# 1/rms on GpSimd by a power, its diagonal products on ScalarE, and a bound that joins the next product, in a one-core encoder block

## The chip, the cores and the metric

The kernel runs on one core of a Trainium2 chip. A core has TensorE (matrix products, PE in the profile; PEld is its loading of weights), VectorE (DVE), ScalarE (ACT), GpSimd (POOL) and SyncE (SP, which here only starts transfers). The metric is the device time of one execution in microseconds; compared are medians of several runs.

## The reference

Two inputs, one of 512 tokens and one of 1024, pass through one encoder layer of width 1024, all in 32-bit floats:

```
h    = rmsnorm(x, norm_mix);   q, k, v, xr, gate = split(h @ w_in)
o    = rmsnorm(diff_attention(q, k, v), subln_g) * 0.8        # 4 heads of 128
xc   = depthwise conv of width 4 over tokens of xr
hl   = rg_lru(xc, forward) + rg_lru(xc, backward)
x    = x + concat(o, hl * gelu(gate)) @ w_out
h2   = rmsnorm(x, norm_ffn)
x    = x + (silu(h2 @ w_gate) * (h2 @ w_up)) @ w_down
out  = rmsnorm(x, norm_final)

rmsnorm(x, g) = x * rsqrt(mean(x * x) + 1e-6) * g
rg_lru: r, i = sigmoids of block products of xc;  a = exp(-8 r softplus(-lambda))
        h_t = a_t h_(t-1) + sqrt(max(1 - a_t^2, 1e-12)) * i_t * xc_t
```

## The kernel before

Activations lie transposed: features on the 128 partitions, tokens along the columns, in blocks of 512 tokens (block 0 is the short input, 1 and 2 the long one). Each 32-bit operand is split into a high part and a remainder (ScalarE rounds, `wh`, `xh`, `hp`; VectorE or GpSimd subtracts, `wl`, `xl`), and each product is three matmuls (`mm3`, L222 to L224).

The work is staged so that TensorE always has a dense product: the input projection of block 0 (`proj`) with the attention of the short input (`attention`) and the recurrent branch (`lru`) beside it; the input projection of blocks 1 and 2; the output projection (`out_proj`); gate and up projections of the short input beside the attention of the long one; then the long input's feed-forward part with sums of halves (`pair_products`), whose sums and differences GpSimd makes (`minus`, L691); and the down projection with the final norm (`finish`). The side work is written as generators that `advance` steps by costs set by hand. That gives the order of the program text; each engine's queue is then laid out by the framework when the kernel is built, by its own scheduling, so that instructions of other stages stand between those of one function. Each engine runs its queue in order.

The norm is made in the same way at 18 places. For the ten RMS norms, squares are added up by VectorE, and `inv_rms_cols` brings the sum over features to one column for each 128 tokens by tiny matmuls with ones (`ss`, L288). VectorE scales it and adds 1e-6 (`ve`, L290). `rsqrt_cols` makes 1/sqrt from it with an integer guess and three Newton steps: eleven VectorE operations on 2, 4 or 8 columns (`rs`, `rt`, L257 to L262). The eight head norms of the attention make their own mean (`ov`, L570) and call `rsqrt_cols` too. `bcast_cols` turns each column into a diagonal matrix (VectorE, `dg`, L270, two buffers) and multiplies it by a matrix of ones (TensorE, `bc`, L271), which gives 1/rms along the tokens on all partitions.

In `lru`, VectorE bounds 1 - a^2 from below (L463), ScalarE takes the root with a factor 0.25 under it (L464, with a load of another table ahead), and VectorE multiplies (L466) and scans (L469).

Of the kernel before, what the change touches and what calls it, by code (L numbers as in the profile page):

```python
# [11 lines left out]
F32 = mybir.dt.float32  # L12
F32R = mybir.dt.float32r
I32 = mybir.dt.int32
F16 = mybir.dt.float16
AF = mybir.ActivationFunctionType
ALU = mybir.AluOpType
# [3 lines left out]
P = 128  # L21
D = 1024
# [8 lines left out]
EPS = 1e-6  # L31
# [57 lines left out]

def build(tc, io, es):  # L90
    nc = tc.nc
    V, A, T = nc.vector, nc.scalar, nc.tensor
    VG = (nc.vector, nc.gpsimd)

    def pool(stack, name, bufs=1, **kw):
        return stack.enter_context(tc.tile_pool(name=name, bufs=bufs, **kw))

    cp = pool(es, "const")
# [11 lines left out]
    def small(n, name, bufs=2):  # L110
        return smp.tile([P, n], F32, name=name, tag=name, bufs=bufs)
# [8 lines left out]
    def bank(name, tag):  # L120
        return banks[tag].tile([P, BLK], F32, name=name, tag=tag)
# [13 lines left out]
    ident = cp.tile([P, P], F32, name="ident")  # L135
    nc.scalar.dma_start(ident, io["ident"])
    onesq = cp.tile([P, P], F32, name="onesq")
    V.memset(onesq, 1.0)
    ones = onesq[:, 0:1]

    warm = cp.tile([P, 1], F32, name="warm")
    A.activation(warm, ones, AF.Exp)
# [6 lines left out]
    def split(h, l, src, eng=V):  # L149
        A.copy(h, src)  # L150
        eng.tensor_tensor(l, src, h.bitcast(F32), ALU.subtract)  # L151
# [68 lines left out]
    def mm3(out, wh, wl, ah, al, first, last, more=False):  # L220

        T.matmul(out, lhsT=wh, rhs=ah, start=first, stop=False, skip_group_check=more)  # L222
        T.matmul(out, lhsT=wh, rhs=al, start=False, stop=False, skip_group_check=more)  # L223
        T.matmul(out, lhsT=wl, rhs=ah, start=False, stop=last, skip_group_check=more)  # L224
# [28 lines left out]
    def rsqrt_cols(ve, n, who="m"):  # L253

        r = small(n, f"rs{who}{n}")
        t = small(n, f"rt{who}{n}")
        V.tensor_scalar(t.bitcast(I32), ve.bitcast(I32), 1, None, ALU.arith_shift_right)  # L257
        V.tensor_scalar(r.bitcast(I32), t.bitcast(I32), -1.0, float(0x5F375A00), ALU.mult, ALU.add)
        for _ in range(3):
            V.tensor_tensor(t, r, r, ALU.mult)  # L260
            V.scalar_tensor_tensor(t, t, -0.5, ve, ALU.mult, ALU.mult)
            V.scalar_tensor_tensor(r, t, 1.5, r, ALU.add, ALU.mult)  # L262
        return r

    def bcast_cols(tag, r, c0, who="m", n=4):

        bc = bank("bc", tag)
        for i in range(n):
            dg = small(P, "dg")
            V.tensor_scalar(dg, ident, r[:, c0 + i:c0 + i + 1], None, ALU.mult)  # L270
            T.matmul(bc[:, i * P:(i + 1) * P], lhsT=onesq, rhs=dg, start=True, stop=True)  # L271
        return bc[:, 0:n * P]

# [10 lines left out]
    def inv_rms_cols(tag, acc, n=4):  # L284

        ss = bank("ss", tag)
        for i in range(n):
            T.matmul(ss[:, i:i + 1], lhsT=acc[:, i * P:(i + 1) * P], rhs=ones, start=True, stop=True)  # L288
        ve = small(n, f"ve{n}")
        V.tensor_scalar(ve, ss[:, 0:n], 1.0 / D, EPS, ALU.mult, ALU.add)  # L290
        return rsqrt_cols(ve, n)

    def inv_rms(tag, acc, n=4):

        return bcast_cols(tag, inv_rms_cols(tag, acc, n), 0, n=n)
# [11 lines left out]
    def load_block(b, other=None, xring="raw"):  # L307
# [32 lines left out]
        if b == 0:  # L340
            for c in range(KC):
                square(c)
        r = inv_rms_cols("lru", acc)
        if b:
            yield YL
        bc = bcast_cols("lru", r, 0)
        rows[b] = rings["rows"](HALF, f"rms{b}")
        A.copy(rows[b], bc)
# [55 lines left out]
    def lru(s, ready):  # L404
        n = length[s]
        nb = n // BLK
        z = n / SEQ_S

        for _ in range(4):
            while not ready:  # L410
                yield 0.5
            c, xr, gt = ready.pop(0)
            gr = rings["lh"]((P, 4, P), "gr")
            nc.sync.dma_start(gr, io["w_gates"][c].rearrange("p (k m) -> p k m", k=4))
            gh = rings["lh"]((P, 4, P), "gh", F32R)
            gl = rings["lh"]((P, 4, P), "gl", F32R)
            split(gh, gl, gr)
            xc = rings["lru"]([P, n], "xcv")

            def col(o):  # L420
                return par[:, o:o + 1]

            A.activation(xc, xr[:, 0:n], AF.Identity, scale=col(C_CW + 4 * c), bias=col(C_CB + c))
            for j in range(1, 4):
                V.scalar_tensor_tensor(xc, xr[:, j:j + n], col(C_CW + 4 * c + j), xc, ALU.mult, ALU.add)
                yield 1.5 * z
            xh = rings["lru"]([P, n], "xch", F32R)
            xl = rings["lru"]([P, n], "xcl", F32R)
            split(xh, xl, xc)
            yield 1.2 * z  # L430
            hs = []
            for dirs in ((0, 1),) if n == BLK else ((0,), (1,)):
                m = len(dirs)

                def tiles(name):
                    t = rings["lru"]([P, m, n], name)
                    return t, [t[:, i] for i in range(m)]


                t2, tr = tiles("tr")  # L440
                b2, bv = tiles("ti")
                for i, d in enumerate(dirs):
                    k = 4 * d + c
                    for b in range(nb):
                        w = slice(b * BLK, (b + 1) * BLK)
                        for t, g, o in ((tr, 0, 0), (bv, 1, 8)):
                            pr = bank("pr", "lru")
                            mm3(pr, gh[:, 2 * d + g], gl[:, 2 * d + g], xh[:, w], xl[:, w], True, True)
                            A.activation(t[i][:, w], pr, AF.Tanh, scale=0.5, bias=hb[:, k + o:k + o + 1])
                            yield YG  # L450
                a2, av = tiles("a")
                for i, d in enumerate(dirs):
                    k = 4 * d + c
                    A.activation(av[i], tr[i], AF.Exp, scale=n4sp[:, k:k + 1], bias=n4sp[:, k:k + 1])
                    A.activation(tr[i], tr[i], AF.Tanh, scale=p4sp[:, k:k + 1], bias=p4sp[:, k:k + 1])
                    V.scalar_tensor_tensor(bv[i], bv[i], 1.0, xc, ALU.add, ALU.mult)
                    for b in range(nb):
                        w = slice(b * BLK, (b + 1) * BLK)
                        sq = rings["lh"](HALF, "sqg")
                        A.activation(sq, av[i][:, w], AF.Square)  # L460
                        V.scalar_tensor_tensor(tr[i][:, w], sq, 1.0, tr[i][:, w], ALU.add, ALU.mult)
                    yield 2.0 * z
                V.tensor_scalar(t2, t2, 1e-12, None, ALU.max)  # L463
                A.activation(t2, t2, AF.Sqrt, scale=0.25)  # L464
                yield 1.0 * z
                V.tensor_tensor(b2, b2, t2, ALU.mult)  # L466
                for i, d in enumerate(dirs):
                    o = slice(None, None, -1) if d else slice(None)
                    V.tensor_tensor_scan(bv[i][:, o], av[i][:, o], bv[i][:, o], 0.0, ALU.mult, ALU.add)  # L469
                hs += bv  # L470
                yield 1.9 * z * m
            V.tensor_tensor(hs[0], hs[0], hs[1], ALU.add)

            ge = rings["lru"]([P, n], "ge")
            A.activation(ge, gt, AF.Square)
            V.scalar_tensor_tensor(ge, ge, 1.0 / GELU_A, gt, ALU.add, ALU.mult)
            A.activation(ge, ge, AF.Tanh, scale=GELU_C * GELU_A)
            V.scalar_tensor_tensor(ge, ge, 1.0, gt, ALU.add, ALU.mult)
            yield 3.0 * z
            V.scalar_tensor_tensor(ge, hs[0], 0.5, ge, ALU.mult, ALU.mult)  # L480
            nc.scalar.dma_start(cat[s][4 + c], ge)
            yield 2.7 * z
# [9 lines left out]
    def attention(s, done, vo):  # L492
# [3 lines left out]
        for hd in range(NH):  # L496
# [112 lines left out]
            yield YV  # L609
            late.pop()()  # L610
            r = rsqrt_cols(ve, nk, "a")
            yield YV * z
            for g in range(n // BLK):
                w = slice(g * BLK, (g + 1) * BLK)
                bc = bcast_cols("pv", r, 4 * g, "a")
                V.scalar_tensor_tensor(ot[:, w], ot[:, w], subg, bc, ALU.mult, ALU.mult)
                nc.scalar.dma_start(cat[s][hd][:, w], ot[:, w])
                yield 1.5
# [68 lines left out]
    def parts_of(rs, w):  # L687
        return [Part(f"b{i}{w}", r, w) for i, r in enumerate(rs)]
# [148 lines left out]
    n = (B1 + B2 + 3 + GRP) // 2  # L837
# [91 lines left out]
    b11, b21, b22, t4, t1, t2, t3 = parts_of(["main"] * 4 + ["pg"] * 3, BLK)  # L929
# [305 lines left out]
```

## Time and profile before

| | |
|---|---|
| median of 3 runs | 1801.11 us (1796.82 to 1801.77) |
| profiled execution | 1798.27 us, its span 1796.5 us |
| TensorE, loading of weights | 1743.1 us (97%), 1434.9 us (80%) |
| VectorE, ScalarE, GpSimd | 1331.4 us (74%), 827.2 us (46%), 256.5 us (14%) |
| mean granted clock of TensorE | 0.989 |

The span is the time from the first to the last instruction of one execution that the profiler recorded. A busy share is an average over stages that are limited by different things. Ends of matmuls are modelled and matmuls overlap, so TensorE's 97% is a share of time with work in it. The granted clock is the share of full speed at which TensorE was allowed to run.

### The profile page before, as it was taken

What the parts mean: (1) busy time and instruction counts of PE and PEld (TensorE: products, weight loads), DVE (VectorE), ACT (ScalarE), POOL (GpSimd) and SP (SyncE); (2) the same over time, 40 slices, a digit from 0 to 9 for tenths busy, and PEclk for the clock granted to TensorE, in tenths of its full rate; (3) what the DMA queues carried; (4) which work ended last, traced back from release to release, by engine and by line L of the source; (5) the groups of instructions that cost most, each with busy time, mean ns of one, the idle gap of its engine ahead of it and who ended that gap; (6) DMA issues with size and microseconds to landing.
All of it is one profiled execution on the core that took longest, in us unless ns stands there. A gap on an engine that the chain in (4) does not pass through costs nothing.

```text
span 1796.5 us, 22898 instructions
## 1 busy us (share of the span) xinstructions
PE 1743.1 (97%) x8316; PEld 1434.9 (80%) x8316; DVE 1331.4 (74%) x2154; ACT 827.2 (46%) x1327; POOL 256.5 (14%) x165
## 2 busy tenths in 40 slices
PE   8999999999999999999999979999999999998997
PEld 7777787777888888888788768888888888887797
DVE  6789878777587778786544996767766766989884
ACT  6568556665355545554323432332233334444451
POOL 0000000000000000000000362323322310555200
PEclk9999999999999999999999989999999999999998
DMA  8633424153473222222555642223332239532361
GB/s 291 198 102 111 142 87 135 66 179 119 145 218 114 86 89 93 70 88 71 196 167 180 205 142 100 100 94 106 110 108 100 100 122 369 170 112 70 99 207 54
DMA packets 105026, 238.79 MB, mean 133 GB/s; under 512 B 12240, under 2 KB 21200, under 8 KB 104912
## 3 DMA queue, kind: packets, MB, share of 16 engines
q1 hardware_dynamic: 76608, 185.04, 32.3%
q10 hardware_dynamic: 28304, 52.28, 7.6%
q8 instruction: 65, 1.06, 0.2%
q14 instruction: 49, 0.40, 0.1%
HBM read 180.00 MB, written 57.28 MB: 132 GB/s over the span
## 4 chain that ended last, share of the span: by engine, by line
PE 79%; DVE 10%; ACT 4%; issue 3%; DMA 3%; POOL 1%; ACTq 0%; SPq 0%; DVEq 0%; POOLq 0%
PE gu L222 5%; PE gu L224 4%; PE gu L223 4%; PE pm L223 4%; PE pm L222 4%; PE pm L224 4%; PE acc L223 3%; PE acc L222 3%; PE acc L224 3%; PE y L224 3%; PE y L222 3%; PE y L223 3%; PE sc L591 2%; PE po L223 2%; PE sc L592 2%
## 5 line engine op out<-in xcount | busy, mean ns | idle before, releaser
L222 PE MATMUL pm<-xh,wh 128*128 128x512 f32 x480 | 189.9, 396 | 5.7 <-ACT wh L209 3.3
L223 PE MATMUL pm<-xl,wh 128*128 128x512 f32 x480 | 189.2, 394 | 1.1 <-DVE xl L336 1.1
L224 PE MATMUL pm<-xh,wl 128*128 128x512 f32 x480 | 189.1, 394 | 0.3 <-DVE wl L210 0.3
L209 ACT CAST wh<-wr 128x1024 fp32r<-128x1024 f32 x100 | 104.8, 1048 | 148.5 <-PE gu L223 62.4
L151 POOL TENSOR_TENSOR ws<-wr,ws 128x512 fp32r<-128x512 f32 x8 | 12.7, 1582 | 1013.2 <-ACT ws L150 1013.2
L223 PE MATMUL acc<-hp,ws 128*128 128x512 f32 (+1 forms) x396 | 142.8, 361 | 6.3 <-DVE hp L151 6.3
L222 PE MATMUL acc<-hp,ws 128*128 128x512 f32 (+1 forms) x396 | 143.2, 362 | 2.8 <-ACT hp L150 2.8
L224 PE MATMUL acc<-hp,ws 128*128 128x512 f32 (+1 forms) x396 | 142.5, 360 | 0.6 <-DVE ws L151 0.6
L222 PE MATMUL gu<-yh,wh 128*128 128x512 f32 x352 | 142.0, 403 | 0.9 <-DVE ev L384 0.9
L224 PE MATMUL gu<-yh,wl 128*128 128x512 f32 x352 | 139.0, 395 | 0.0
L223 PE MATMUL gu<-yl,wh 128*128 128x512 f32 x352 | 138.6, 394 | 0.0
L210 DVE TENSOR_TENSOR wl<-wr,wh 128x1024 fp32r<-128x1024 f32 x100 | 122.2, 1222 | 17.6 <-ACT wh L209 16.9
L597 ACT ACTIVATE pb<-pb,mn 128x1024 f32<-128x1024 f32 (+1 forms) x96 | 96.9, 1009 | 73.5 <-DVE mn L594 73.4
L151 DVE TENSOR_TENSOR hp<-hr,hp 128x512 fp32r<-128x512 f32 (+1 forms) x143 | 111.0, 787 | 26.3 <-ACT hp L150 22.4
L594 DVE CUSTOM_DVE_ANT_0 pb<-sc,tab 128x1024 f32<-128x1024 f32 (+1 forms) x96 | 100.1, 1043 | 33.1 <-PE sc L592 31.6
L713 ACT CAST ws<-s 128x512 fp32r<-128x512 f32 x88 | 54.7, 622 | 131.1 <-PE y L224 48.1
L222 PEld LDWEIGHTS pm<-xh,wh 128*128 128x128 f32 x480 | 90.6, 189 | 24.5 <-ACT wh L209 3.5
L150 ACT CAST hp<-hr 128x512 fp32r<-128x512 f32 (+1 forms) x143 | 77.2, 550 | 71.0 <-PE acc L224 24.1
L223 PEld LDWEIGHTS pm<-xl,wh 128*128 128x128 f32 x480 | 90.5, 189 | 19.8 <-DVE xl L336 1.8
L224 PEld LDWEIGHTS pm<-xh,wl 128*128 128x128 f32 x480 | 90.6, 189 | 19.4 <-DVE wl L210 1.0
L713 ACT CAST ws<-wr 128x512 fp32r<-128x512 f32 x66 | 41.1, 622 | 111.1 <-PE y L224 38.2
L223 PEld LDWEIGHTS acc<-hp,ws 128*128 128x128 f32 x396 | 76.3, 193 | 18.1 <-DVE hp L151 7.4
(271 smaller groups left out, 4604.6 us busy)
## 6 DMA issues: line engine op xcount, KB each, us to landing
wr<-w_gate SPq DMA_DIRECT2D x44, 512.0 KB, 3.5
wr<-w_up SPq DMA_DIRECT2D x44, 512.0 KB, 3.5
wr<-w_in SPq DMA_DIRECT2D x40, 512.0 KB, 4.1
hr<-hs SPq DMA_DIRECT2D x77, 256.0 KB, 2.8
hs<-t ACTq DMA_DIRECT2D x44, 256.0 KB, 2.0
hs<-ht ACTq DMA_DIRECT2D x33, 256.0 KB, 2.9
wr<-w_out SPq DMA_DIRECT2D x16, 512.0 KB, 3.6
xd<-xh ACTq DMA_DIRECT2D x28, 256.0 KB, 2.5
```

The source lines that it names most:

```text
L150: A.copy(h, src)
L151: eng.tensor_tensor(l, src, h.bitcast(F32), ALU.subtract)
L209: A.copy(h, r)
L210: V.tensor_tensor(l, r, h.bitcast(F32), ALU.subtract)
L222: T.matmul(out, lhsT=wh, rhs=ah, start=first, stop=False, skip_group_check=more)
L223: T.matmul(out, lhsT=wh, rhs=al, start=False, stop=False, skip_group_check=more)
L224: T.matmul(out, lhsT=wl, rhs=ah, start=False, stop=last, skip_group_check=more)
L591: T.matmul(sc[:, w], lhsT=qh[m][:, qs], rhs=K[m][:, w], start=True, stop=False)
L592: T.matmul(sc[:, w], lhsT=ql[m][:, qs], rhs=K[m][:, w], start=False, stop=True)
L594: V.tensor_tensor_reduce(out=pp[m], in0=sc, in1=tab[:, 896 - q0:896 - q0 + n], scale=-0.125, scalar=3e38, op0=ALU.add, op1=ALU.min, accum_ ...
L597: A.activation(pp[m], pp[m], AF.Exp, scale=-1.0, bias=mn, accum_out=zz)
L713: A.copy(h[:, 0], src)
```

## The change

1/rms is now made by GpSimd: a power with the exponent -0.5 from a constant tile, and one Newton step, five operations in place of eleven on VectorE. The scaling ahead of it (`ve`) and the diagonal products move from VectorE to ScalarE. In the recurrent branch the bound is no longer an operation of its own under the root: the root's result, which carries a factor of a half, is bounded by 5e-7 in the product that follows. Two constants are set at the start.

```diff
+    V, A, T, G = nc.vector, nc.scalar, nc.tensor, nc.gpsimd
...
+    eps = cp.tile([P, 1], F32, name="eps")
+    V.memset(eps, EPS)
+    mhalf = cp.tile([P, 8], F32, name="mhalf")
+    V.memset(mhalf, -0.5)
...
-        V.tensor_scalar(t.bitcast(I32), ve.bitcast(I32), 1, None, ALU.arith_shift_right)
-        V.tensor_scalar(r.bitcast(I32), t.bitcast(I32), -1.0, float(0x5F375A00), ALU.mult, ALU.add)
-        for _ in range(3):
-            V.tensor_tensor(t, r, r, ALU.mult)
-            V.scalar_tensor_tensor(t, t, -0.5, ve, ALU.mult, ALU.mult)
-            V.scalar_tensor_tensor(r, t, 1.5, r, ALU.add, ALU.mult)
+        G.tensor_tensor(r, ve, mhalf[:, 0:n], ALU.pow)
+        G.tensor_tensor(t, r, r, ALU.mult)
+        G.tensor_tensor(t, t, ve, ALU.mult)
+        G.tensor_scalar(t, t, -0.5, 1.5, ALU.mult, ALU.add)
+        G.tensor_tensor(r, t, r, ALU.mult)
...
-            V.tensor_scalar(dg, ident, r[:, c0 + i:c0 + i + 1], None, ALU.mult)
+            A.activation(dg, ident, AF.Copy, scale=r[:, c0 + i:c0 + i + 1])
...
-        V.tensor_scalar(ve, ss[:, 0:n], 1.0 / D, EPS, ALU.mult, ALU.add)
+        A.activation(ve, ss[:, 0:n], AF.Identity, scale=1.0 / D, bias=eps)
...
-                V.tensor_scalar(t2, t2, 1e-12, None, ALU.max)
                 A.activation(t2, t2, AF.Sqrt, scale=0.25)
...
-                V.tensor_tensor(b2, b2, t2, ALU.mult)
+                V.scalar_tensor_tensor(b2, t2, 5e-7, b2, ALU.max, ALU.mult)
```

## Rows read from the trace of the kernel before

**Rows 1.** The page: busy time, share of the span and instructions of each engine.

```profile
PE 1743.1 (97%) x8316; PEld 1434.9 (80%) x8316; DVE 1331.4 (74%) x2154; ACT 827.2 (46%) x1327; POOL 256.5 (14%) x165
```

**Rows 2.** Waits of TensorE: us in total, times, longest us.

```profile
PE bc L271 <- DVE dg L270: 8.8, 9, 4.0
```

**Rows 3.** Timeline, TensorE: start, us, instruction, idle before it and its releaser.

```profile
572.58 0.68 PE L271 MATMUL bc<-dg,onesq 128*128 128x128 f32 x4 [0.35 <-DVE dg L270]
```

**Rows 4.** Timeline around 981 us, VectorE, GpSimd and TensorE.

```profile
985.34 0.16 DVE L290 TENSOR_SCALAR ve<-ss 128x4 f32<-128x4 f32 x1
...
987.49 1.22 DVE L260 TENSOR_TENSOR rtm<-rsm 128x4 f32<-128x4 f32 x1
...
986.97 1.73 POOL L151 TENSOR_TENSOR ws<-wr,ws 128x512 fp32r<-128x512 f32 x1 [15.14 <-ACT ws L150]
...
991.27 0.68 PE L271 MATMUL bc<-dg,onesq 128*128 128x128 f32 x4 [3.97 <-DVE dg L270]
```

**Rows 5.** Windows: us, engines' busy us and instructions, granted clock, DMA share, GB/s.

```profile
175.00:181.00 6.00, 5.67 (x17) 3.86 (x18) 5.86 (x9) 4.52 (x6) 0.00 (x0) 0.72 0.40 131
...
991.00:996.00 5.00, 4.73 (x18) 4.05 (x19) 3.83 (x9) 0.30 (x2) 0.00 (x0) 0.66 0.83 276
```

**Rows 6.** Timeline around 170 us, TensorE and ScalarE.

```profile
170.88 0.71 PE L271 MATMUL bc<-dg,onesq 128*128 128x128 f32 x4 [0.21 <-DVE dg L270]
174.85 0.50 PE L222 MATMUL pm<-xh,wh 128*128 128x512 f32 x1 [3.26 <-ACT wh L209]
...
172.77 0.56 ACT L348 COPY rms<-bc 128x512 f32<-128x512 f32 x1
...
173.77 1.03 ACT L209 CAST wh<-wr 128x1024 fp32r<-128x1024 f32 x1
```

**Rows 7.** Timeline of the end, all engines.

```profile
1785.43 0.16 DVE L290 TENSOR_SCALAR ve<-ss 128x2 f32<-128x2 f32 x1 [0.70 <-PE ss L288]
...
1787.60 0.16 DVE L262 SCALAR_TENSOR_TENSOR rsm<-rtm,rsm 128x2 f32<-128x2 f32 x1
1787.80 0.48 DVE L270 TENSOR_SCALAR dg<-ident,rsm 128x128 f32<-128x128 f32 x2
1788.23 1.19 PE L271 MATMUL bc<-dg,onesq 128*128 128x128 f32 x4 [2.84 <-DVE dg L270]
1789.46 0.37 ACT L1104 COPY bcs<-bc 128x256 f32<-128x256 f32 x1 [5.67 <-PE bc L271]
...
1789.91 1.41 POOL L1108 TENSOR_TENSOR xr<-xr,bcs 128x256 f32<-128x256 f32 x2 [116.69 <-ACT bcs L1104]
```

**Rows 8.** VectorE by line and shape: busy us, mean ns | idle before.

```profile
L466 DVE TENSOR_TENSOR ti<-ti,tr 128x1024 f32<-128x1024 f32 x12 | 14.7, 1223 | 5.3 <-ACT tr L464 5.2
L270 DVE TENSOR_SCALAR dg<-ident,rsa 128x128 f32<-128x128 f32 x48 | 12.1, 284 | 5.5 <-PE bc L271 5.3
...
L463 DVE TENSOR_SCALAR tr<-tr 128x1024 f32<-128x1024 f32 x12 | 8.3, 691 | 0.2
...
L480 DVE SCALAR_TENSOR_TENSOR ge<-ti,ge 128x1024 f32<-128x1024 f32 x4 | 4.9, 1220 | 0.0
```

**Rows 9.** ScalarE by line and shape, the same columns.

```profile
L335 ACT ACTIVATE xh<-xc,par 128x512 fp32r<-128x512 f32 x24 | 16.0, 713 | 6.2 <-DMA xc<-xt 6.2
...
L1084 ACT ACTIVATE xr<-xr,par 128x256 f32<-128x256 f32 x1 | 0.5, 492 | 0.0
...
L171 ACT ACTIVATE tmp<-tmp 128x2 f32<-128x2 f32 x1 | 0.2, 204 | 2.2 <-DVE tmp L180 2.2
```

**Rows 10.** GpSimd: two lines' durations (ns min/median/max), and two dependent instructions.

```profile
L1108 POOL TENSOR_TENSOR xr<-xr,bcs x2: 727/728/728, 1789.9 to 1790.6; 128x256 f32<-128x256 f32 x2
...
L691 POOL TENSOR_TENSOR t3r<-y,y x2: 2399/2614/2830, 1019.9 to 1034.9; 128x1024 f32<-128x1024 f32 x2
...
1055.85 2.28 POOL L706 TENSOR_TENSOR s<-wr 128x512 f32<-128x512 f32 x1
1058.21 2.16 POOL L691 TENSOR_TENSOR s<-s,wr 128x512 f32<-128x512 f32 x1
```

More of the change, by code (lines that the diff above doesn't have):

```diff
@@ L91, in build @@
     nc = tc.nc
-    V, A, T = nc.vector, nc.scalar, nc.tensor
+    V, A, T, G = nc.vector, nc.scalar, nc.tensor, nc.gpsimd
     VG = (nc.vector, nc.gpsimd)
```

## The prediction

> **What bounds the kernel now.** I read the page first: TensorE is busy 1743.1 us of a span of 1796.5 us, VectorE 74%, ScalarE 46%, GpSimd 14% [rows 1]. So at most 53.4 us can be had without fewer matmuls, and an edit that only lightens VectorE is worth what it takes out of TensorE's gaps. Next the waits of TensorE: the broadcast matmuls of 1/rms (`bc`, L271) wait 8.8 us for VectorE's diagonal products in 9 gaps, the longest of them 4.0 us [rows 2]. That is the whole of what TensorE visibly waits for at the place that the change rebuilds; the reader should keep 8.8 beside the 1796.5.
>
> Then I went through the 18 places where 1/rms is made (ten RMS norms of L290, eight head norms of the attention), in order of time, and looked at what lies between the column sums and `bc`. They fall into three kinds.
>
> Most are like the one at 570 us: TensorE has other matmuls to do while VectorE works, and then stands for a few tenths, here 0.35 us [rows 3]. Fifteen of the 18 are of this kind, from nothing to 0.5 us each. TensorE arrives at `bc` about when the old chain is done, so a shorter chain saves a little there, and a longer one costs nearly all of its lengthening.
>
> Two are pockets. At 981 us VectorE reaches `ve` only at 985.34, since its queue holds other work, and its chain is then held up: one tiny product takes 1.22 us while GpSimd runs a 1.73 us subtraction; TensorE stands 3.97 us in front of `bc` [rows 4]. Behind such an idle stretch TensorE runs slowly: the granted clock from 991 to 996 us is 0.66, so 0.34 x 5 = 1.7 us more is lost [rows 5]. At 170 us VectorE and ScalarE are both full, `bc` ends at 171.6, ScalarE copies the row at 172.77, splits the next weights at 173.77, and TensorE starts again at 174.85 after 3.26 us idle [rows 6]; the clock from 175 to 181 us is 0.72, another 1.7 us [rows 5].
>
> The last is the end, where nothing else is left: from `ve` at 1785.43 to `bc` at 1788.23 everything is on the path [rows 7].
>
> **The change, part by part.**
>
> *The chain, alone.* Today: `ve` at 1785.43, eleven VectorE operations until 1787.76, a diagonal product that ends about 0.28 us after 1787.80, that is 1788.08 [rows 7, 8]: 2.65 us. Afterwards: `ve` on ScalarE, for which the nearest row is a two-column activation of 0.20 us [rows 9]; a hop to GpSimd of 0.08 us (ScalarE's copy of 1789.46 ends at 1789.83, GpSimd starts at 1789.91) [rows 7]; five GpSimd operations. Their price has to be extrapolated: a 128x256 product takes 0.727 us, a 128x1024 difference 2.399 us when nothing disturbs it, so (2.399 - 0.727) / 768 = 0.00218 us a column and 0.727 - 256 x 0.00218 = 0.17 us fixed; four columns cost 0.18 us. Between two dependent ones lie 0.08 us (1055.85 + 2.28 to 1058.21) [rows 10]. Five plain ones: 5 x 0.18 + 4 x 0.08 = 1.22 us. Then the product on ScalarE: with a scale per partition 128x512 takes 0.713 us and 128x256 0.492 us, so 128x128 about 0.38 us [rows 9]. Sum: 0.20 + 0.08 + 1.22 + 0.38 = 1.9 us, 0.75 us less than today, if the power is priced like a product.
>
> *The power.* No row shows it. From below it costs what a product costs, 0.18 us. From above I take the dearest undisturbed GpSimd row, 1024 columns in 2.40 us [rows 10], though two to eight columns need hardly be so dear. I take 0.5 us, under the 0.73 us of 256 columns. The chain is then 2.2 us, 0.4 us shorter than today; with 2.40 us it is 4.1 us, 1.5 us longer.
>
> *At the end of the kernel*: -0.4 us (bounds -0.75 and +1.5).
>
> *The pocket at 981.* `ve` leaves VectorE's queue, so it no longer stands behind the subtractions there; ScalarE's queue waits for the same loads, though, and GpSimd has its own 1.73 us subtraction at 986.97, behind or ahead of which the new chain is placed. If it goes ahead, `bc` comes 3 to 4 us earlier and the clock stays up: up to 4.0 + 1.7 = 5.7 us. If it goes behind, it starts at 988.7 and `bc` follows at about 990.9, nearly as today. I take -2.5 us.
>
> *The pocket at 170.* VectorE loses the chain of one head norm and four diagonal products, about 2.2 + 4 x 0.28 = 3.3 us, and the 0.69 us bound of L463 [rows 8]; but four products of 0.38 us come to ScalarE, which is as full, and the last link here is ScalarE's split of the weights. Bounds 0 and -(3.3 + 1.7) = -5.0; I take -2.0 us.
>
> *The other fifteen places.* TensorE has no slack to speak of there. The chain being 0.4 us shorter would give at most 0.35 us each; against it, ScalarE takes `ve` and four products in order between its own casts, the long ones 1.03 us [rows 6], so each of the two new visits can wait for one of them. The other way round, `ve` waits for TensorE's column sums and the first product for GpSimd, and behind them in ScalarE's queue stand the casts of the next weights and activations, for which TensorE waits next; with a chain of 2 us such a hold is short, with 4 us it is not. In a broadcast of four, VectorE's products are already paced by their two buffers, so ScalarE's 0.38 us loses little. I take +0.06 us each, +0.9 us in all (bounds -5, +23 with the dearest power).
>
> *ScalarE and VectorE in total.* 84 products of 0.38 us put 32 us on an engine that is 46% busy; VectorE is freed of 84 x 0.28 = 24 us, 18 chains of about 2.2 us = 40 us and the bounds. Outside the places above TensorE does not wait for them, so this is costed at nothing; the cover is TensorE's own queue, and if ScalarE's casts came late instead, each would cost up to its own 1.03 us.
>
> *The bound under the root.* L463 goes: 12 x 0.691 us of VectorE. L466 becomes a form with a scalar, 1.22 us as L480 is, against 1.223 us for the plain product [rows 8]. The root starts up to 0.69 us earlier, in a branch that runs beside the matmuls: nothing, apart from the pocket at 170. The two new constants are tiny and lie in the start.
>
> Sum: -0.4 - 2.5 - 2.0 + 0.9 = -4.0 us. The profiled execution took 1798.27 us (span 1796.5 and 1.8 around it), so 1794.3; the median of the runs lies 2.8 us above that execution, so **1797 us**.
>
> **A rule against it.** [Rows 4] show VectorE's 0.16 us operation stretched to 1.22 us while GpSimd works, and GpSimd's own operation at 1.73 us, over the 1.29 us that 512 columns cost by the line above. The Trainium skill (SBUF — State Buffer, Who interferes with whom) states the reason: a VectorE instruction with two SBUF inputs and a GpSimd instruction that reads SBUF exclude each other, and the second "fully blocks". The trace agrees. By the row for an undisturbed operation the sum is the one above; by the rule the new chain is priced by VectorE's traffic, and the time is that of the third rival.
>
> **The rivals.**
> 1. *Both pockets open.* VectorE's relief lets the chain start at once at 981 and moves the whole stretch at 170: -5.7 - 5.0 = -10.7, with the end -11: 1790. For it: both stand behind VectorE's queue. Against: ScalarE and the loads are late there too.
> 2. *It does nothing.* The chain is as long as before, since two visits to ScalarE eat what GpSimd saves, and the pockets are bound by the loads and ScalarE: -1 to +2, so 1801.
> 3. *GpSimd is held by VectorE.* As VectorE's product was held in [rows 4], each of the five short operations comes upon a running VectorE operation of 0.7 to 1.2 us, then upon the next. It decides where VectorE has no gaps, about eight of the places; five waits of 0.35 us are 1.8 us each, less the 0.4: 8 x 1.4 = +11 us, 1812. Against: at the other half of the places, as at the end, VectorE has nothing else to do.
> 4. *The power is slow*, and this is the one on the other side: at 2.40 us the chain is 1.5 us longer, at 17 places without slack 26 us: 1823 with the pockets' gain, 1827 without. From about 0.9 us on the change loses at the end.
>
> **How the numbers follow.** Forecast (-1 to -7) 0.32; rival 1 0.22; rival 2 0.22; rival 3 0.12; rival 4 0.12. A change of 0.3% (5.4 us) is about what a measurement tells from none. Faster: nearly all of rival 1 and a quarter of the forecast, 0.30. Slower: rivals 3 and 4 nearly whole, 0.23. Same: 0.47. The range runs from 1788, which takes in rival 1 almost whole, to 1812, rival 3; rival 4 and the tails stay out, 0.2. Since both signs are in it: the likeliest case alone is 1794 to 1800.
>
> **What would show it.** At the end `ve` to `bc` should take 2.4 us instead of 2.8, with GpSimd operations of 0.2 us about 0.08 us apart and a power under 0.7 us. At 981 us the wait at `bc` should be about half of 4.0; at 170 us the idle stretch shorter than 3.3. TensorE's total wait at `bc` should fall below 8.8 us. If the power takes over 0.9 us, or GpSimd's short operations wait for VectorE by half a microsecond each, or if the order in which the build places the new instructions puts `ve` or the products behind ScalarE's casts, the forecast is wrong on the slow side; if the clock never drops at 991 and 175, on the fast one.

## The result: 1.7% slower

The changed kernel takes 1830.26 us (median of 4, 1823.37 to 1833.09) against 1800.86; the ratio is 1.0166, interval 1.015 to 1.0182. The prediction was 1797 us in a range from 1788 to 1812. The profiled execution has a span of 1830.6 us, 34.1 us more than before.

The page of the changed kernel, busy time of each engine:

```profile
PE 1758.3 (96%) x8316; PEld 1439.3 (79%) x8316; DVE 1266.4 (69%) x1852; ACT 856.3 (47%) x1421; POOL 296.3 (16%) x255
```

VectorE got the relief that the change is built on, 65 us. TensorE has the same 8316 matmuls as in [rows 1], but is busy 15 us longer and idle 19 us longer. Both halves will matter.

The waits of TensorE in the changed kernel, us in total, times, longest:

```profile
PE bc L274 <- ACT dg L273: 26.4, 19, 2.7
PE acc L227 <- DVE hp L155: 5.8, 3, 3.0
PE sc L227 <- DVE hp L155: 5.7, 2, 4.1
PE sc L226 <- ACT hp L154: 5.4, 1, 5.4
```

The wait at the broadcast of 1/rms is 26.4 us where [rows 2] have 8.8. The place of [rows 3], the first head norm of the long input, in the timeline of the changed kernel:

```profile
576.66 0.61 PE L568 MATMUL pv<-onesq,osq 128*128 128x1 f32 x4
577.13 0.47 PE L226 MATMUL gu<-yh,wh 128*128 128x512 f32 x1
577.44 0.39 PE L227 MATMUL gu<-yl,wh 128*128 128x512 f32 x1
577.67 0.40 PE L228 MATMUL gu<-yh,wl 128*128 128x512 f32 x1
577.90 0.40 PE L226 MATMUL gu<-yh,wh 128*128 128x512 f32 x1
578.14 0.39 PE L227 MATMUL gu<-yl,wh 128*128 128x512 f32 x1
578.36 0.40 PE L228 MATMUL gu<-yh,wl 128*128 128x512 f32 x1
580.87 0.78 PE L274 MATMUL bc<-dg,onesq 128*128 128x128 f32 x4 [2.11 <-ACT dg L273]
...
577.62 1.64 POOL L261 TENSOR_TENSOR rsa<-ov,mhalf 128x8 f32<-128x8 f32 x1 [161.82 <-DVE ov L573]
579.33 0.20 POOL L262 TENSOR_TENSOR rta<-rsa 128x8 f32<-128x8 f32 x1
579.61 0.20 POOL L263 TENSOR_TENSOR rta<-rta,ov 128x8 f32<-128x8 f32 x1
579.90 0.20 POOL L264 TENSOR_SCALAR rta<-rta 128x8 f32<-128x8 f32 x1
580.19 0.20 POOL L265 TENSOR_TENSOR rsa<-rta,rsa 128x8 f32<-128x8 f32 x1
```

Two things are to be seen. The power takes 1.64 us for eight columns; the other four operations take 0.20 each. And between the column sums (`pv`) and `bc` stand six matmuls, as at the three other head norms of the long input. In the kernel before, 11, 20, 19 and 19 stood there. The third of these places in the kernel before, with 16 of its 19 matmuls left out:

```profile
759.94 0.50 PE L565 MATMUL pv<-onesq,osq 128*128 128x1 f32 x4
760.30 0.49 PE L222 MATMUL gu<-yh,wh 128*128 128x512 f32 x1
...
764.30 0.39 PE L224 MATMUL gu<-yh,wl 128*128 128x512 f32 x1
764.53 0.39 PE L222 MATMUL gu<-yh,wh 128*128 128x512 f32 x1
765.01 0.68 PE L271 MATMUL bc<-dg,onesq 128*128 128x128 f32 x4
```

The chain from the first of its operations to the last, 577.62 to 580.39 in the changed kernel, is 2.77 us, and as long at the three others; the eleven VectorE operations took 2.2 us at the first place and 3.8 at the three others. So at three of four places the new chain is shorter than the old one. TensorE still waits 2.1 us at all four (2.09 to 2.13), where it waited 0.35 us at the first and at most 0.1 at the others: it comes to `bc` earlier.

Behind the wait TensorE runs slowly, as it did in [rows 5]. The window in the changed kernel: us, engines' busy us, granted clock, DMA share, GB/s.

```profile
581.00:586.00 5.00, 5.00 (x21) 4.31 (x22) 1.91 (x3) 3.09 (x8) 0.00 (x0) 0.66 0.14 52
```

A clock of 0.66 is a mean over five microseconds, of a part at 1.2 GHz and the rest at 2.4. The second and the third of the four waits are followed by 0.66 as well; behind the fourth, which is no shorter, it stayed at 1.00.

At the end, which answers to [rows 7], the chain came out nearly as long as before, `ve` to `bc` 2.63 us in place of 2.80:

```profile
1820.01 0.26 ACT L293 ACTIVATE ve<-ss,eps 128x2 f32<-128x2 f32 x1 [1.64 <-PE ss L291]
1820.35 0.69 POOL L261 TENSOR_TENSOR rsm<-ve,mhalf 128x2 f32<-128x2 f32 x1 [24.15 <-ACT ve L293]
1821.13 0.19 POOL L262 TENSOR_TENSOR rtm<-rsm 128x2 f32<-128x2 f32 x1
...
1821.95 0.20 POOL L265 TENSOR_TENSOR rsm<-rtm,rsm 128x2 f32<-128x2 f32 x1
1822.18 0.69 ACT L273 ACTIVATE dg<-ident,rsm 128x128 f32<-128x128 f32 x2 [1.91 <-POOL rsm L265]
1822.64 0.58 PE L274 MATMUL bc<-dg,onesq 128*128 128x128 f32 x1 [2.66 <-ACT dg L273]
```

In what follows a stage is measured from the start of its first matmul to the start of its last. In the stage that holds the four head norms of the long input (the short input's gate and up projections), TensorE takes 401.4 us before and 414.9 us after.

### The profile page after: what moved, and what is told of

It reads as the page before. It is cut to its first block, busy times and chain, and to the rows that moved or that the text cites. A ratio compares the mean times of both kernels' runs of the same rounds, so it can differ in the third digit from the quotient of the medians.

```text
span 1830.6 us, 22782 instructions
## 1 busy us (share of the span) xinstructions
PE 1758.3 (96%) x8316; PEld 1439.3 (79%) x8316; DVE 1266.4 (69%) x1852; ACT 856.3 (47%) x1421; POOL 296.3 (16%) x255
## 4 chain that ended last, share of the span: by engine, by line
PE 79%; DVE 7%; ACT 5%; POOL 3%; DMA 3%; issue 3%; SPq 0%; ACTq 0%; DVEq 0%; POOLq 0%
PE gu L226 4%; PE gu L228 4%; PE gu L227 4%; PE pm L227 4%; PE pm L226 4%; PE pm L228 4%; PE y L227 3%; PE y L226 3%; PE y L228 3%; PE acc L227 3%; PE acc L228 3%; PE acc L226 3%; PE x L226 2%; PE z L228 2%; PE x L227 2%
## 5 line engine op out<-in xcount | busy, mean ns | idle before, releaser
L227 PE MATMUL acc<-hp,ws 128*128 128x512 f32 (+1 forms) x396 | 144.3, 365 | 5.8 <-DVE hp L155 5.8
L226 PE MATMUL acc<-hp,ws 128*128 128x512 f32 (+1 forms) x396 | 144.5, 365 | 2.2 <-ACT hp L154 2.2
L228 PE MATMUL acc<-hp,ws 128*128 128x512 f32 (+1 forms) x396 | 144.4, 365 | 0.2 <-DVE ws L155 0.2
L261 POOL TENSOR_TENSOR rsa<-ov,mhalf 128x4 f32<-128x4 f32 (+1 forms) x8 | 10.9, 1366 | 647.4 <-DVE ov L573 647.4
```

What stands on the lines that cost most here:

```text
L261: G.tensor_tensor(r, ve, mhalf[:, 0:n], ALU.pow)
```

## The experiments

Theory A: the build lays the broadcast too early into TensorE's queue for what the chain takes on the chip. Rivals: B, ScalarE's new work delays its casts; C, VectorE holds GpSimd's operations. Two more, D and E, came up on the way.

**E1. A product in place of the power.**

```diff
-    V.memset(mhalf, -0.5)
+    V.memset(mhalf, 1e-9)
...
-        G.tensor_tensor(r, ve, mhalf[:, 0:n], ALU.pow)
+        G.tensor_tensor(r, ve, mhalf[:, 0:n], ALU.mult)
```

> The changed kernel with its power replaced by a plain product with a constant of 1e-9 of the same shape, so its outputs are not 1/rms; every queue's order stays that of the changed kernel. Theory A (TensorE reaches the broadcast 6 to 18 matmuls behind the column sums and then waits for a chain of 2.1 to 2.8 us, in which the power takes 0.7 to 1.6): the chain falls to about 1.3 us, the waits at the broadcast from 26 to about 10 us, the slow-clock stretches behind them go, 1806 to 1812 us. Rival B (the work moved to ScalarE delays its casts, the power is not the matter): within 4 us of 1830. Rival C (GpSimd's short operations are held by VectorE): five operations still wait, at least 1822.

1811.91 us, ratio 1.0079 (1.0064 to 1.0095). The queues are those of the changed kernel, so the build had made no more room for a power than for a product; on the chip the product takes 0.20 us. What this kernel leaves out is 1/rms itself: its values are near zero.

```profile
572.10 0.20 POOL L261 TENSOR_TENSOR rsa<-ov,mhalf 128x8 f32<-128x8 f32 x1 [160.53 <-DVE ov L573]
...
573.24 0.20 POOL L265 TENSOR_TENSOR rsa<-rta,rsa 128x8 f32<-128x8 f32 x1
```

TensorE's wait at `bc` fell from 26.4 to 16.2 us, and the stage of the four head norms to 403.2 us, nearly that of before. It falls by 11.7 us though the four powers are only 4 x 1.44 = 5.8 us shorter; most of the rest is the slow clock that no longer follows (1.00 behind all four places). That other values alone raise the clock is a rival here; E12, whose values are right, settles it for this stage. So the power is most of the loss, but 14 us stay that A had not named.

**E2. The broadcast later, by pacing.**

```diff
-YV, YF, YL, YT = 1.0, 1.5, 3.0, 1.5
+YV, YF, YL, YT = 1.0, 4.0, 3.0, 4.0
...
             r = rsqrt_cols(ve, nk, "a")
-            yield YV * z
+            yield 4.0 * z
```

> The changed kernel with more pacing steps between the chain and the broadcast in the head norms and the two last norms, so that the broadcast stands 13 to 42 matmuls behind the column sums at ten places instead of 6 to 18; the operations are the same. Theory A: the waits at those places go, though the power is as slow as before: 1806 to 1812 us. A theory that says the slow power costs its own length wherever it stands: 1827 to 1833. Rival B: within 4 us of 1830.

1826.5 us, ratio 1.0159 (1.0138 to 1.018): a miss. In the stage of the long input's head norms A holds: 404.7 us in place of 414.9, the power as slow as before (1.64 us), and 18 matmuls ahead of the first `bc`, which then doesn't wait (at the three others 13 to 18, and waits of 0.7 us at most):

```profile
584.17 0.39 PE L228 MATMUL gu<-yh,wl 128*128 128x512 f32 x1
584.40 0.61 PE L274 MATMUL bc<-dg,onesq 128*128 128x128 f32 x4
```

But the later steps stand in the short input's side work and in the last norms too, and other stretches grew: the one from 153 us to the short input's output projection took 210.1 us (205.2 in the changed kernel, 199.5 before), and the one from the first down projection to the end of the long input's sums of halves took 4 us more than in the changed kernel. That the work put off is the reason was not shown apart. It is tried again, for the long input alone, in E12.

**E3 and E4. The chain alone, and the rest alone.** E3 is the kernel before with the power and the Newton step on GpSimd; E4 the changed kernel with the eleven operations back.

```diff
# E3, of the change only this (and the two constants)
-        V.tensor_scalar(t.bitcast(I32), ve.bitcast(I32), 1, None, ALU.arith_shift_right)
...
+        G.tensor_tensor(r, ve, mhalf[:, 0:n], ALU.pow)
...
+        G.tensor_tensor(r, t, r, ALU.mult)
# E4, all of the change but this
```

> The kernel before with the power and the Newton step on GpSimd alone; the scaling and the diagonal products stay on VectorE and the bound under the root stays. Theory A: the broadcasts stand 6 to 11 matmuls behind the sums, so nearly the whole loss is here: 1822 to 1832 us. Rival B: 1799 to 1804.

> The changed kernel with the eleven operations of 1/sqrt back on VectorE; the scaling and the diagonal products stay on ScalarE and the bound stays in the product. Theory A: 1796 to 1804 us, the waits at the broadcast near the 9 us of the kernel before. Rival B: most of the loss, over 1815.

E3: 1826.7 us, ratio 1.0159 (1.0144 to 1.0175), TensorE's wait at `bc` 27.4 us. E4: 1813.22 us, ratio 1.0087 (1.0072 to 1.0102), its wait 13.4 us. E3 is as A says. E4 is a miss for A and for B: half of the loss, and its wait at `bc` explains only 4.6 of its 15 us. E3 and E4 together lose more than the change: something is in both. In E4 the first norm alone costs TensorE 3.9 us, and here B's mechanism is seen, as a part:

```profile
27.75 1.23 DVE L214 TENSOR_TENSOR wl<-wr,wh 128x1024 fp32r<-128x1024 f32 x1 [0.22 <-ACT wh L213]
28.89 0.15 DVE L266 SCALAR_TENSOR_TENSOR rsm<-rtm,rsm 128x4 f32<-128x4 f32 x1
...
29.41 1.00 ACT L165 ACTIVATE d<-d 128x960 f16<-128x960 f32 x1 [1.70 <-DMA d<-dist]
30.32 0.68 ACT L274 ACTIVATE dg<-ident,rsm 128x128 f32<-128x128 f32 x2
...
30.76 0.78 PE L275 MATMUL bc<-dg,onesq 128*128 128x128 f32 x4 [3.90 <-ACT dg L274]
```

1/rms is there at 29.04, and the product stands in ScalarE's queue behind an operation that makes the distance table (`d`) and waits for its load: 1.28 us until it starts at 30.32, where the kernel before needed 0.56. The larger part is VectorE's own queue, which was laid out anew too: other operations, like `wl` above, stand between the eleven, and 1/rms is done 3.0 us later than in the kernel before (26.02).

**E5. The kernel before again.**

> The kernel before, once more, for the size of what a repeat alone moves. All theories: 1794 to 1801 us, and in each stage within 1 us of the first profile; where a stage differs by more, that much isn't put down to an edit.

1797.49 us, ratio 0.9993 (0.9984 to 1.0002). Every stage is within 1.2 us of the first profile, so stages can be compared to about that.

**E6 and E7. The bound alone, and ScalarE's part alone**, each in the kernel before, each with the two constants (`eps`, `mhalf`) of the change.

```diff
# E6
-                V.tensor_scalar(t2, t2, 1e-12, None, ALU.max)
...
-                V.tensor_tensor(b2, b2, t2, ALU.mult)
+                V.scalar_tensor_tensor(b2, t2, 5e-7, b2, ALU.max, ALU.mult)
# E7
-            V.tensor_scalar(dg, ident, r[:, c0 + i:c0 + i + 1], None, ALU.mult)
+            A.activation(dg, ident, AF.Copy, scale=r[:, c0 + i:c0 + i + 1])
...
-        V.tensor_scalar(ve, ss[:, 0:n], 1.0 / D, EPS, ALU.mult, ALU.add)
+        A.activation(ve, ss[:, 0:n], AF.Identity, scale=1.0 / D, bias=eps)
```

> The kernel before with the bound under the root moved into the product, and nothing else. Theory A as it stands after e4 (the 15 us of the rest come from ScalarE's part): 1795 to 1800 us. Rival D (any edit in the recurrent branch shifts the order that the build lays out in later stages, and that alone costs): 1804 to 1814, with the loss behind 980 us, where the recurrent branch has long ended.

> The kernel before with the scaling and the diagonal products on ScalarE, the eleven operations on VectorE and the bound under the root as before. Theory A: 1808 to 1816 us, as e4, the loss where ScalarE's products come behind its casts. Rival D: 1796 to 1804, with the loss of e4 in the bound's part.

E6: 1803.99 us, ratio 1.0028 (1.0016 to 1.0039). E7: 1816.15 us, ratio 1.0095 (1.008 to 1.0111). E6 loses where D says, behind 890 us, in stages that the edit doesn't touch. But D's reason is not what the trace shows: TensorE has no more gaps there. Its matmuls follow each other more slowly. In 80 us of unbroken 512-column matmuls, the window of TensorE alone (us, busy us and matmuls, granted clock, DMA share, GB/s), first in the kernel before:

```profile
1520.00:1600.00 80.00, 80.00 (x354) 1.00 0.54 173
```

and in E6, at the same clock:

```profile
1520.00:1600.00 80.00, 80.00 (x349) 1.00 0.55 187
```

That is 226 ns for one and 229. The changed kernel and E1, E3 have 349 as well. What all of them share is the two constants, which take 64 bytes at the front of SBUF; every tile that is placed behind them from the left edge moves, while those that the code places from the right edge stay: theory E. E7 ends at the upper edge of what A said; how much of it is ScalarE's part is taken up behind E9 and E10.

**E8. Two powers.**

```diff
         G.tensor_tensor(r, ve, mhalf[:, 0:n], ALU.pow)
+        G.tensor_tensor(r, ve, mhalf[:, 0:n], ALU.pow)
```

> The changed kernel with a second power of the same inputs right behind the first, at all 18 places. Theory A: the broadcasts move back by at most two matmuls, TensorE waits for nearly the whole of it, 13 x 1.1 + 4 x 1.6 less a little, plus a slow-clock stretch at more places: 1844 to 1858 us. Rival B and C: within 5 us of 1830.

1852.13 us, ratio 1.0292 (1.0278 to 1.0306), in the middle of what A said. The wait at `bc` is now 42.9 us; the first head norm of the long input waits 3.6 us with seven matmuls ahead of it. A second power costs 22 us, a second time what the first did and a little more.

**E9 and E10. 64 bytes, with the queues unchanged.** Before the other tiles of the left side lies one that nothing uses. E9 makes it 64 bytes longer in the kernel before; E10 makes it 64 bytes shorter in the changed kernel, which undoes the constants' shift. In both, each engine's queue holds the same instructions in the same order as in the kernel that it comes from.

```diff
# E9, in the kernel before
-    pool(es, "edge_left").tile([P, 32], F32, name="edge_left")
+    pool(es, "edge_left").tile([P, 48], F32, name="edge_left")
# E10, in the changed kernel
-    pool(es, "edge_left").tile([P, 32], F32, name="edge_left")
+    pool(es, "edge_left").tile([P, 16], F32, name="edge_left")
```

> The kernel before with its unused tile at the left edge of SBUF 64 bytes longer, so that all that is placed behind it moves by 64 bytes; every queue holds the same instructions in the same order. Theory E (the two new constants move the matmuls' operands by 64 bytes, which lengthens the pitch of the later stages' matmuls from 226.9 to 230.0 ns, some 9 us in all of the edits so far): 1805 to 1811 us with that pitch. Rival (the longer pitch comes from the new order of the queues): 1796 to 1801 with a pitch of 227.

> The changed kernel with that unused tile 64 bytes shorter, which takes the two constants' shift back; the order of every queue is that of the changed kernel. Theory E: the pitch of the later stages is 227 ns again and the time 1817 to 1824 us; what stays over the kernel before, some 22 us, are the waits at the broadcast. Rival: 1827 to 1833.

E9: 1807.07 us, ratio 1.0043 (1.0026 to 1.0059). E10: 1820.01 us, ratio 1.0121 (1.0106 to 1.0135). The same window, E9 and then E10:

```profile
1520.00:1600.00 80.00, 80.00 (x349) 1.00 0.59 204
```

```profile
1520.00:1600.00 80.00, 80.00 (x355) 1.00 0.66 235
```

Theory E is shown both ways: 8 us added by moving tiles alone, 8 to 10 us taken away by moving them back, with the matmul rate to match. The data traffic of the window doesn't order them: E10 moves the most, 235 GB/s, and has the most matmuls. The shift is also what E3 and E4 both hold, and so count twice. (The 226.9 and 230.0 ns of the expectations are means over the starts of all such matmuls of these stages; in E9 and E10 they are 230.0 and 226.9.) What is left in E10, 21.5 us of span, stands in the stages with norms: 10.7 us at the long input's head norms, 5.3 between 153 us and the short input's output projection, 5.3 from the long input's down projection to the end. Its wait at `bc` is 27.3 us.

With E9 the loss of E7 can be told apart by stages, though no run was made for it. Of E7's 17.1 us of span, 9.8 come from the short input's output projection on, where E9 loses 10.3; 7.5 stand before it, in the input projections, where E9 loses nothing. So some 7 us of E7 go with ScalarE's part. In E10 all these early stages together lose 3.9 us.

**E11 and E12. The bound without the constants, and a late broadcast without the shift.** E11 is E6 without the two constants. E12 is E10 with the later steps of E2, but only in the head norms of the long input and in `finish`.

```diff
# E12
-YV, YF, YL, YT = 1.0, 1.5, 3.0, 1.5
+YV, YF, YL, YT = 1.0, 4.0, 3.0, 1.5
...
-            yield YV * z
+            yield (4.0 if n > BLK else YV) * z
```

> The kernel before with the bound in the product alone, without the two constants, so nothing moves in SBUF. Theory E: e6 without the longer pitch, 1791 to 1797 us, as the recurrent stage was 3 us shorter in e6. Rival: 1801 to 1806, as e6.

> The changed kernel with the shift taken back and the broadcast later in the long input's four head norms and in the last norms, by more pacing steps there. Theory A with E: 1830 less 10 for the pitch, 10 for the long input's attention and 3 at the end: 1803 to 1811 us; a broadcast that is late enough takes the power's price away, so it still doesn't beat the kernel before. If the power's length had to be paid wherever the broadcast stands: 1817 or more.

E11: 1796.94 us, ratio 0.9986 (0.9977 to 0.9995), the one version below the kernel before, by 0.14%, where a mere repeat (E5) came out 0.07% below; without the two constants E6's edit is 7 us faster than with them. E12: 1807.68 us, ratio 1.0046 (1.0031 to 1.0062). The stage of the long input's head norms takes 403.8 us in E12 and 412.1 in E10, with a power no faster. So in this stage the power's length is not the price; the place of the broadcast in TensorE's queue is. Of the 8 us of span that E12 stays over the kernel before, 2.4 are in that stage, 3.3 before the short input's output projection, where no step was added, and 1.8 from the long input's down projection on.

**E13 to E15. Other shifts**, in the kernel before: the unused tile 64 bytes shorter, 128 longer, 32 longer (`[P, 16]`, `[P, 64]`, `[P, 40]`).

> The kernel before with the unused tile 64 bytes shorter; the queues hold the same instructions in the same order. If the placement matters by its distance modulo 128 bytes, this is as e9: 1805 to 1810 us and 349 matmuls in the 80 us where the kernel before has 354. If it matters by where in SBUF something ends or crosses, it may be as before: 1796 to 1801.

> The same tile 128 bytes longer. Distance modulo 128 bytes: 1796 to 1801 us and 354 matmuls in that stretch. A cost that grows with the shift: over 1808.

> The same tile 32 bytes longer. Distance modulo 64 bytes can't be told by shifts of 64 and 128: if only a half step of 64 matters, this lies between, 1799 to 1806 us; if any shift off the old place costs alike, 1805 to 1810.

Ratios 1.0038 (1.0023 to 1.0053), 1.0038 (1.0023 to 1.0052) and 1.0063 (1.0048 to 1.0078), with 351, 349 and 349 matmuls in the 80 us. A distance modulo 64 or 128 bytes doesn't explain that: all four shifts that were tried cost, 32 bytes as much as any. The place of the kernel before is a good one among these five; why, and for which operand, stays open. Since the tiles of the right side stay where they are, each shift also changes the distance between the two sides; no run separates the two.

## Why the prediction was wrong, by its own steps

- *"TensorE arrives at `bc` about when the old chain is done", so a chain 0.4 us shorter changes little: the fifteen other places, +0.9 us.* This is the step that failed first. It took the broadcast's place in TensorE's queue for given. The build laid it out anew, six to eighteen matmuls behind the sums nearly everywhere, with no more room for a power than for a product (E1: the same queues). The wait at `bc` rose by 17.6 us, to which the slow clock behind it adds (E1: 11.7 us for 5.8 us of power in one stage). Shown by E1, E2 and E12 in the long input's stage, E3 and E8. With the tiles moved back, E10 loses 21 us, of which 18.5 are longer waits at `bc`; at the places outside the long input's head norms a later broadcast was tried with the tiles moved back only in `finish`.
- *"The two new constants are tiny and lie in the start."* Wrong as a term of the sum: not their time, but their 64 bytes cost 8 to 10 us, by slower matmuls in stages with no edit (E9, E10); by their size they are most of the 14 us that E1 leaves. The unused tile at the edge of SBUF stood in the code and was not asked about.
- *The power at 0.5 us.* Inside its bounds, mis-sized: 0.69 us for two columns, 1.01 for four when undisturbed, 1.64 for eight. The power grows with the columns, about 0.16 us each; the plain operations, expected at 0.18, took 0.20.
- *The chain, alone.* The mechanism held. At the end of the kernel `ve` to `bc` is 0.17 us shorter, not 0.4, and nearly all of the difference is the power (0.69 for 0.5).
- *The pocket at 981.* About as forecast: the wait at `bc` is 1.97 us where [rows 4] have 3.97, and the clock falls all the same.
- *The pocket at 170.* The gain did not come: TensorE stands 2.69 us there, at 182.56, now for VectorE, against 3.26 in [rows 6], and the slow clock follows as before.
- *The bound under the root: nothing apart from that pocket.* Right in size: E11 is 2 us below the kernel before, hardly more than the repeat's 1.3.
- *ScalarE's load costed at nothing.* Not so in E7, where some 7 us in the input projections go with it, by stages. At the first norm of E4, ScalarE's queue holds the product back by 0.7 us more than VectorE's did; the rest of the 3.9 us there is VectorE's queue. How much it costs in the changed kernel itself stays open: that place waits 1.2 us there, and E3, without ScalarE's part, loses 5.8 us in the same stages, E10 3.9.
- *Rival 3.* Seen, and small. The GpSimd groups of the changed kernel by shape (busy us, mean ns, idle):

```profile
L261 POOL TENSOR_TENSOR rsm<-ve,mhalf 128x4 f32<-128x4 f32 x8 | 10.4, 1298 | 268.0 <-ACT ve L293 268.0
...
L262 POOL TENSOR_TENSOR rtm<-rsm 128x4 f32<-128x4 f32 x8 | 3.0, 380 | 0.6
...
L262 POOL TENSOR_TENSOR rtm<-rsm 128x2 f32<-128x2 f32 x2 | 0.4, 193 | 0.2
```

  The first product of a four-column chain takes 0.38 us in the mean of eight, one of them 1.08, where one costs 0.20 in quiet stages, and the power 1.30 where 1.01 is its least: some half a microsecond a chain, not the 1.8 us of that rival. Each of the ten short operations that take over 0.3 us overlaps a VectorE operation with two tensors as inputs and ends 0.05 to 0.06 us behind it. The Trainium skill's rule (SBUF — State Buffer, Who interferes with whom) is borne out; its price here is small.
- *Rival 4*, a slow power at places without slack, came closest in place and sum (1823 to 1827), but its reason for "without slack" was the old queue, so that its sum comes near is luck. At three of the long input's four head norms the old queue had 19 or 20 matmuls there, 4.3 us at 0.227 each, for a chain that now needs 3.6 us from the sums to `bc`.

## What to carry to other kernels

A build that lays out the queues by itself may leave no more room for a slow operation than for a quick one (E1). The harm is then done where its consumer is put: compare the number of matmuls between producer and consumer before and after, and if it shrank, push the consumer back by hand, place by place, since a step that puts off other work too can cost what it gains (E2). Before adding even one small constant, look at what it moves in memory; take its bytes from padding, as E10 does, and compare the spacing of matmuls in a stage that the edit doesn't touch. A relief for an engine that TensorE doesn't wait for is worth little here: VectorE has 65 us less work in the changed kernel, and E10, which has the same queues with the tiles moved back, is still 21 us slower than the kernel before.

## What was not expected of the hardware

- The spacing of unbroken 512-column matmuls at the full granted clock depends on where their tiles lie in SBUF: 354 in 80 us at the old place, 349 to 351 after shifts of -64, +32, +64 and +128 bytes, with every queue the same.
- A GpSimd power costs several times a product: 1.64 us against 0.20 for 128x8, 0.69 against 0.19 for 128x2.
- A wait of 2 us can cost TensorE more than itself: behind three of the four waits of 2.1 us at the long input's head norms the granted clock is 0.66 over 5 us, as it was behind the 4 us of [rows 4]; behind the fourth it is 1.00.
